# One decoder layer: fewer steps of norm work beside each down-projection tile, a final norm that loads h once, one more step ahead of the broadcasts of a norm, and a weight tile of odd SSM batches in other buffers

## The chip, the cores and the metric

The kernel runs on one core of one Trainium2 chip. The metric is the device time of one execution in microseconds. Three runs of the kernel before gave 2239.86, 2243.06 and 2243.66 us, median 2243.06. The engines are TensorE (PE), VectorE (DVE), ScalarE (ACT), GpSimd (POOL) and SyncE (SP), which issues most of the transfers; each works through its own queue in order, and semaphores tie the queues together.

## The reference

One layer over 2064 tokens (16 meta tokens and 2048), 1024 wide, in float32:

```
hn   = rms_norm(h, norm_mix_g);  proj = hn @ w_in        # b, c, v, u: 512 columns each
conv = b * causal_dwconv3(c * v)
ssm  = g * sigmoid(g @ w_glu),  g = gelu(S5 state space of u)
h    = h + concat(rms_norm(conv), rms_norm(ssm)) @ w_out
up   = causal_dwconv3(rms_norm(h, norm_ffn_g) @ w_up) + bias     # 2 x 2816 columns
h    = h + (silu(a) * val) @ w_down
y    = rms_norm(h, norm_final_g)[meta positions removed]
```

Weights and activations are multiplied as a high part and a low part each, three matmuls for every product: high by high, low by high, high by low.

## The kernel before

The tokens are cut into six pieces of 344, two to a block, and channels lie on the partitions. The program runs through these stages:

1. The input projection of every block, and beside it the SSM in eight batches of four channel groups. For each batch `ssm_load_out` (L699) loads a tile `mo` with the output matrices (512 KB), and `ssm_out` (L772) multiplies it: the matmuls `py` at L781 by `ub` (the input) and at L782 by `sb` (the states that VectorE has scanned). ScalarE evicts them with the gelu into `gb`, and `gb` goes out to DRAM as `g_d`.
2. The first half of the output projection of block 0, whose operands come from the convolution (`pk`, in `conv_part`, eight tiles of 24 matmuls). Meanwhile `g_d` comes back by tokens as four tiles `gt`. ScalarE and VectorE make its high and low parts `gh`, `gl` (L970), and the half-GLU (`glu_block`) multiplies them by `w_glu` into `pg`.
3. The norms of the SSM and conv outputs (names with `ms` and `mc`), the output projection of the three blocks (`po`), and the residual, which `xr` collects and which is written to DRAM as `h_d`.
4. The MLP, three blocks one after the other. `up` does one of 22 pairs of 128 rows of w_up in seven products (matmuls at L1349 to L1351 into `xy` and `pz`, evictions `z`, from L1387 on), then the conv, silu and product. The pairs come in chunks of 4, 4, 4, 3, 3 and 4. After the first pair of a chunk the eight down tiles (`dn`) of the chunk before it are multiplied, evicted (`ev`, L1446) and added to `h_d` by an accumulating transfer.
5. The final norm of a block (`finish`), beside the MLP of the next, and for block 2 at the end (`finish_last`).

A norm is a generator. It squares the input, sums over features with a matmul by ones (`st`, L188), takes the power on GpSimd and multiplies the identity by the result on VectorE (`dg`, three pieces, L203). A matmul by ones then spreads the rows over all partitions (`sb`, L206), and ScalarE copies that out (`rs`). `inv_rms_from` (L214) first loads its input from `h_d` into tiles `sq_f` or `sq_y`, and ScalarE squares them in place.

Such generators wait in a queue called `prep`. The main code calls `prep.step(n)` at fixed places, between projection tiles and after a down tile, and every step runs the generator up to its next `yield`. The number of yields between two parts of a norm therefore sets how much main work lies between them. A second number, the lanes, says how many generators go on in one step. The scheduler then puts each engine's instructions in the order of these calls, as far as the data allow.

Weights are loaded ahead through SP into raw tiles (`wr`), and split by a copy on ScalarE (`wh`, L247) and a subtraction on VectorE (`wl`, L109). Line 109 is the helper for all tensor-tensor operations on VectorE.

Buffers are named by tag and handed on in turn. The tag `sq` has four buffers in the MLP; the loads of the norms, the y tiles and the operands of the next block use them. The tag `ut` has two buffers, through which u is written to DRAM in the first stage.

Of the kernel before, what the change touches and what calls it, by code (L numbers as in the profile page):

```python
# [17 lines left out]
P = 128  # L18
# [39 lines left out]
def layer_kernel(ctx, tc, xq, pk, w_in, w_glu, w_out, w_up, w_down, ssm_s, ssm_m, y):  # L58
# [49 lines left out]
    def tt(out, a, b, op):  # L108
        V.tensor_tensor(out, a, b, op=op)  # L109
# [83 lines left out]
    def inv_rms_at(ss, starts, nfeat, n, name, out=None, keep=False):  # L193
# [8 lines left out]
        for j, o in enumerate(starts):  # L202
            V.tensor_scalar(dg[:sl, o : o + sl], ident[:sl, :sl], r[:sl, j : j + 1], None, op0=ALU.mult)  # L203
        yield
        pb = aux_tile(f"sb_{name}")
        T.matmul(pb[:, :n], ones[:sl, :], dg[:sl, :n], start=True, stop=True)  # L206
# [7 lines left out]
    def inv_rms_from(srcs, n, name, out=None):  # L214
# [6 lines left out]
        yield  # L221
        if xg is not None:
            yield
            yield
        for t in ts:
# [65 lines left out]

    prep, ssm = Side(), Side()
    SQ = 2

# [404 lines left out]
    def ssm_load_out(b):  # L699
        g0 = b * GB  # L700
        mo = a1.tile([P, GB, 2, P], F32, tag="mo", name=f"mo_{b}")
        dma(out=mo, in_=mat_d[:, g0 : g0 + GB, 1:3, :])
        mos[b] = mo

# [68 lines left out]
    def ssm_out(b):  # L773
# [3 lines left out]
        for q in range(PB):  # L777
            ps = mm_tile(f"py_{b}_{q}")
            for par in range(2):
                g = 2 * q + par  # L780
                T.matmul(ps[:, par, :NC], mo[:, g, 1, :], ub[:, g, :], start=True, stop=False)  # L781
                T.matmul(ps[:, par, :NC], mo[:, g, 0, :], yy[b][:, q, par, :], start=False, stop=True)  # L782
            S.activation(gb[:, 2 * q : 2 * q + 2, :], ps[:, :, :NC], AF.Gelu_apprx_tanh)
# [251 lines left out]
    prep.add(prep_glu(0, hg[0]), prep_glu(1, hg[1], **xh2))  # L1035
    prep.lanes = 1
    kept = conv_part(0)
# [259 lines left out]
    def finish(b):  # L1297
        for c in range(2):
            s0, n = y_at(b, c)
            srcs = [h_d[:, i * 4 : i * 4 + 4, s0 : s0 + n] for i in range(2)]  # L1300
            rs = yield from inv_rms_from(srcs, n, f"y{b}{c}")
            yield
            for i in range(2):
                a = half_tile(n, f"y_{b}_{c}_{i}", tag="sq", bufs=4)
                dma(out=a, in_=srcs[i])
                yield
                yield
                for k in range(4):
# [27 lines left out]
    for b in range(3):  # L1336
# [119 lines left out]
        for ci, (f0, nk) in enumerate(chunk_of):  # L1456
# [3 lines left out]
            for f in range(f0, f0 + nk):  # L1460
                up(f, f == f0 + nk - 1 and ci == last)
                if f == f0 and ci:
                    for ms in first_pair:
                        down(ci - 1, ms)
                        work()
                        prep.step(2 * len(ms))
            if ci == last:
# [122 lines left out]
```

## Time and profile before

| | us |
|---|---|
| median of three runs | 2243.06 |
| lowest, highest | 2239.86, 2243.66 |
| the profiled execution | 2245.62 |
| its span in the trace | 2243.8 |
| PE, DVE, ACT, POOL busy in it | 2136.4, 1678.8, 1107.1, 151.6 |

Times in the traces count from the start of the span. A line of the list of waits names who waited, for whom, the total, how many times and the longest. A line of the windows table gives, for a stretch of the span, the busy time and the instructions of each engine, then the clock that was granted to TensorE as a share of its full speed, and the share and rate of the transfers. In the timeline, the brackets hold the idle time of the engine before an instruction and what ended it. Names drop their numbers there: `z` stands for every z tile.

### The profile page before, as it was taken

To read this page: it belongs to the slowest core of one execution; us is meant where nothing else is said; L and a number is where in the kernel's file an instruction comes from. 1 tells how busy PE (TensorE), PEld (TensorE's weight loads), DVE (VectorE), ACT (ScalarE), POOL (GpSimd) and SP (SyncE) were. 2 spreads that over 40 slices of the span, in tenths; PEclk is the share of its full clock that TensorE was granted. 3 is DMA by queue.
4 is the path that set the end of the run, shared out by engine and by line. 5 is a ranking of instruction groups with operands and counts; after the bars stand their busy time and mean duration, and the time that the engine had idled before them with its cause. 6 is when DMAs were issued, how large, how long until landed. Compare 5 with 4: busy or idle time off the path is not lost.

```text
span 2243.8 us, 33100 instructions
## 1 busy us (share of the span) xinstructions
PE 2136.4 (95%) x13012; PEld 2072.6 (92%) x13012; DVE 1678.8 (75%) x2495; ACT 1107.1 (49%) x1647; POOL 151.6 (7%) x174
## 2 busy tenths in 40 slices
PE   4999999999899999999999898999999999999997
PEld 3999999989899999999999898999998999999996
DVE  7776498867866797686669686787768779667776
ACT  3234343326523364554556555455555655555554
POOL 0000000000000001101110010100110010110000
PEclk8899999999999999999999999999999999999998
DMA  5475544343376436525554454725554463554463
GB/s 189 119 225 151 144 133 160 129 130 118 107 245 209 139 95 148 122 77 123 131 131 99 135 148 133 202 77 123 129 133 120 126 180 100 131 119 97 101 174 101
DMA packets 174909, 305.85 MB, mean 136 GB/s; under 512 B 32480, under 2 KB 108960, under 8 KB 174624
## 3 DMA queue, kind: packets, MB, share of 16 engines
q1 hardware_dynamic: 154016, 251.98, 36.2%
q0 software_dynamic: 19584, 47.52, 12.6%
q10 hardware_dynamic: 1152, 4.23, 0.5%
q8 instruction: 102, 1.67, 0.3%
q14 instruction: 55, 0.45, 0.1%
HBM read 219.86 MB, written 83.82 MB: 135 GB/s over the span
## 4 chain that ended last, share of the span: by engine, by line
PE 47%; issue 31%; DVE 8%; DMA 7%; POOL 3%; ACT 2%; SPq 0%; POOLq 0%; DVEq 0%; ACTq 0%
PE xy L1349 5%; PE xy L1350 4%; PE xy L1351 4%; PE dn L138 3%; PE dn L139 3%; POOL h_d L1450 3%; PE dn L142 3%; PE pz L1351 2%; PE pz L1350 2%; PE pz L1349 2%; PE po L138 1%; PE po L139 1%; PE po L142 1%; PE pu L139 1%; PE pu L142 1%
## 5 line engine op out<-in xcount | busy, mean ns | idle before, releaser
L109 DVE TENSOR_TENSOR wl_up<-wr_up,wh_up 128x1024 fp32r<-128x1024 f32 x198 | 241.8, 1222 | 155.0 <-ACT wh_up L247 153.1
L138 PE MATMUL dn<-ah,wh_dn 128*128 128x344 f32 (+1 forms) x1024 | 326.9, 323 | 11.7 <-ACT ah L247 8.9
L139 PE MATMUL dn<-al,wh_dn 128*128 128x344 f32 (+1 forms) x1024 | 325.3, 321 | 0.1
L247 ACT ACTIVATE wh_up<-wr_up 128x1024 fp32r<-128x1024 f32 x198 | 209.3, 1058 | 215.1 <-DVE wr_up L109 59.6
L1349 PE MATMUL xy<-h_t,wh_up 128*128 128x344 f32 (+1 forms) x792 | 264.8, 334 | 11.7 <-ACT z L1387 7.3
L1350 PE MATMUL xy<-l_t,wh_up 128*128 128x344 f32 (+1 forms) x792 | 254.9, 322 | 0.0
L1351 PE MATMUL xy<-h_t,wl_up 128*128 128x344 f32 (+1 forms) x792 | 254.6, 321 | 0.0
L142 PE MATMUL dn<-ah,wl_dn 128*128 128x344 f32 (+1 forms) x1024 | 247.1, 320 | 0.0
L138 PEld LDWEIGHTS dn<-ah,wh_dn 128*128 128x128 f32 x1024 | 193.7, 190 | 16.8 <-ACT ah L247 9.7
L1450 POOL DMA_DIRECT2D h_d<-ev x136 | 118.1, 869 | 1271.6 <-ACT ev L1446 1268.3
L139 PEld LDWEIGHTS dn<-al,wh_dn 128*128 128x128 f32 x1024 | 193.9, 189 | 1.3 <-DVE al L109 0.8
L1349 PE MATMUL xy<-h_b,wh_up 128*128 128x344 f32 (+1 forms) x528 | 176.6, 336 | 10.5 <-ACT ev L1446 8.1
L1349 PEld LDWEIGHTS xy<-h_t,wh_up 128*128 128x128 f32 x792 | 150.5, 190 | 30.4 <-ACT z L1394 13.6
L142 PEld LDWEIGHTS dn<-ah,wl_dn 128*128 128x128 f32 x1024 | 177.9, 189 | 0.0
L1350 PE MATMUL xy<-l_b,wh_up 128*128 128x344 f32 (+1 forms) x528 | 169.8, 322 | 0.0
L1351 PE MATMUL xy<-h_b,wl_up 128*128 128x344 f32 (+1 forms) x528 | 168.6, 321 | 0.0
L1350 PEld LDWEIGHTS xy<-l_t,wh_up 128*128 128x128 f32 x792 | 150.9, 191 | 0.0
L1351 PEld LDWEIGHTS xy<-h_t,wl_up 128*128 128x128 f32 x792 | 150.8, 190 | 0.0
L247 ACT ACTIVATE wh_dn<-wr_dn 128x512 fp32r<-128x512 f32 (+1 forms) x144 | 85.5, 594 | 123.5 <-issue 43.5
L115 DVE SCALAR_TENSOR_TENSOR g<-z,pv,g 128x688 f32<-128x688 f32 (+1 forms) x132 | 122.4, 927 | 19.6 <-ACT g L1354 18.9
L109 DVE TENSOR_TENSOR wl_dn<-wr_dn,wh_dn 128x512 fp32r<-128x512 f32 (+1 forms) x144 | 92.5, 645 | 50.8 <-ACT wh_dn L247 49.8
L115 DVE SCALAR_TENSOR_TENSOR v<-z,pneg,v 128x688 f32<-128x688 f32 (+1 forms) x132 | 122.5, 928 | 9.4 <-ACT v L1354 8.2
(394 smaller groups left out, 5377.2 us busy)
## 6 DMA issues: line engine op xcount, KB each, us to landing
wr_up<-in_w_up SPq DMA_DIRECT2D x132, 512.0 KB, 5.2
h_d<-ev POOLq DMA_DIRECT2D x88, 344.0 KB, 7.0
wr_dn<-in_w_down SPq DMA_DIRECT2D x96, 256.0 KB, 2.7
wr_cw<-in_w_in SPq DMA_DIRECT2D x36, 512.0 KB, 4.7
h_d<-ev POOLq DMA_DIRECT2D x48, 336.0 KB, 6.5
x_c<-in_xq SPq DMA_DIRECT2D x16, 688.0 KB, 4.8
wr_dn<-in_w_down SPq DMA_DIRECT2D x48, 192.0 KB, 2.4
xr<-in_xq SPq DMA_DIRECT2D x24, 344.0 KB, 3.9
```

The source lines that it names most:

```text
L109: V.tensor_tensor(out, a, b, op=op)
L115: V.scalar_tensor_tensor(out=out, in0=a, scalar=s, in1=b, op0=ALU.mult, op1=ALU.add)
L138: T.matmul(ps[c], hi[:, k, :], xh, start=k == 0, stop=False)
L139: T.matmul(ps[c], hi[:, k, :], xl, start=False, stop=False)
L142: T.matmul(ps[c], lo[:, k, :], xh, start=False, stop=k == nk - 1)
L247: S.activation(hi, t, AF.Copy)
L1349: T.matmul(ps, hi[:, j, :], xh[:, j, :], start=start and j == 0, stop=False, **kw)
L1350: T.matmul(ps, hi[:, j, :], xl[:, j, :], start=False, stop=False, **kw)
L1351: T.matmul(ps, lo[:, j, :], xh[:, j, :], start=False, stop=j == 3, **kw)
L1450: G.dma_start(out=h_d[:, m, s0 : s0 + no], in_=ev, accum_op=ALU.add)
```

## The change

There are five edits:

1. `mo` of the odd batches is held in two tiles of tag `ut`, for two groups each, and loaded by two transfers; the even batches keep the tile `mo`.
2. A flag `slack`, set at the start of the second stage, adds one `yield` between `dg` and the `sb` matmul in every norm from there on.
3. `inv_rms_from` always yields four times between the issue of its loads and the Squares. Before, it did so only once the MLP's buffers were open, and yielded twice ahead of that.
4. `finish` loads each half of h once, into y tiles, and writes the squares into separate tiles `ysq`, all of tag `sq`. Before, it loaded h into `sq_y`, squared it in place, and loaded h a second time for the scaling. Eight loads fewer are issued.
5. After a down tile beside the next chunk, `prep.step` runs `len(ms)` steps, no longer twice as many.

```
     def inv_rms_at(...):
             V.tensor_scalar(dg[:sl, o : o + sl], ident[:sl, :sl], r[:sl, j : j + 1], None, op0=ALU.mult)
         yield
+        if slack:
+            yield
         pb = aux_tile(f"sb_{name}")
...
     def inv_rms_from(...):
         yield
         yield
-        if xg is not None:
-            yield
-            yield
+        yield
+        yield
         for t in ts:
             S.activation(t, t, AF.Square)
...
     def ssm_load_out(b):
         g0 = b * GB
-        mo = a1.tile([P, GB, 2, P], F32, tag="mo", name=f"mo_{b}")
-        dma(out=mo, in_=mat_d[:, g0 : g0 + GB, 1:3, :])
-        mos[b] = mo
+        if b % 2 == 0:
+            mo = a1.tile([P, GB, 2, P], F32, tag="mo", name=f"mo_{b}")
+            dma(out=mo, in_=mat_d[:, g0 : g0 + GB, 1:3, :])
+            mos[b] = [mo[:, g] for g in range(GB)]
+            return
+        mos[b] = []
+        for i in range(0, GB, 2):
+            t = cvp.tile([P, NJ, 86], F32, tag="ut", bufs=2, name=f"mo_{b}_{i}").rearrange("p j x -> p (j x)")
+            mo = t[:, : 4 * P].rearrange("p (g m c) -> p g m c", g=2, m=2)
+            dma(out=mo, in_=mat_d[:, g0 + i : g0 + i + 2, 1:3, :])
+            mos[b] += [mo[:, 0], mo[:, 1]]
...
-    prep.lanes = 1
+    prep.lanes, slack = 1, True
     kept = conv_part(0)
...
     def finish(b):
         for c in range(2):
             s0, n = y_at(b, c)
-            srcs = [h_d[:, i * 4 : i * 4 + 4, s0 : s0 + n] for i in range(2)]
-            rs = yield from inv_rms_from(srcs, n, f"y{b}{c}")
-            yield
-            for i in range(2):
-                a = half_tile(n, f"y_{b}_{c}_{i}", tag="sq", bufs=4)
-                dma(out=a, in_=srcs[i])
+            xs, sq = ([half_tile(n, f"{k}_{b}_{c}_{i}", tag="sq", bufs=4) for i in range(2)] for k in ("y", "ysq"))
+            for i, a in enumerate(xs):
+                dma(out=a, in_=h_d[:, i * 4 : i * 4 + 4, s0 : s0 + n])
+            for _ in range(4):
                 yield
-                yield
+            for a, q in zip(xs, sq):
+                S.activation(q, a, AF.Square)
+            yield
+            q = sq[0]
+            tt(q, q, sq[1], ALU.add)
+            tt(q[:, 0:2, :], q[:, 0:2, :], q[:, 2:4, :], ALU.add)
+            tt(q[:, 0, :], q[:, 0, :], q[:, 1, :], ALU.add)
+            yield
+            rs = yield from inv_rms_of(q[:, 0, :], D, n, f"y{b}{c}")
+            yield
+            for i, a in enumerate(xs):
                 for k in range(4):
                     V.scalar_tensor_tensor(
...
                         work()
-                        prep.step(2 * len(ms))
+                        prep.step(len(ms))
```

The first place where the order moves is SP's queue at the end of the SSM. `mo_7` is the tile of the last batch, `ub_7` its input, `wr_o` weights of the output projection, `wr_g` those of the GLU, `gt` the gelu's output on its way back. Before:

```order
L696 DMA ub_7_4174<-u_d_69 128x1032
L702 DMA mo_6_4176<-mat_d_74 128x4x256
L119 DMA wr_o004_4341<-in_w_out 128x512
L119 DMA wr_o005_4476<-in_w_out 128x512
L884 DMA mx_d_71<-tc_2_3_4308 128x2x344
L119 DMA wr_o006_4508<-in_w_out 128x512
L702 DMA mo_7_4417<-mat_d_74 128x4x256
L257 DMA x_mc4_0_5691<-mx_d_71 128x4x344
L963 DMA gt_4465<-g_d_70 128x8x258 x4
L119 DMA wr_o007_4541<-in_w_out 128x512
```

After:

```order
L119 DMA wr_o003_4260<-in_w_out 128x512
L698 DMA ub_7_4180<-u_d_69 128x1032
L712 DMA mo_7_0_4423<-mat_d_74 128x2x256
L712 DMA mo_7_2_4425<-mat_d_74 128x2x256
L119 DMA wr_o004_4347<-in_w_out 128x512
L119 DMA wr_o005_4484<-in_w_out 128x512
L894 DMA mx_d_71<-tc_2_3_4314 128x2x344
L119 DMA wr_o006_4516<-in_w_out 128x512
L258 DMA x_mc4_0_5699<-mx_d_71 128x4x344
L119 DMA wr_o007_4549<-in_w_out 128x512
L973 DMA gt_4473<-g_d_70 128x8x258 x4
```

The two halves of mo_7 now stand right behind ub_7, ahead of wr_o004 to wr_o006, and wr_o007 stands ahead of the four gt loads.

The second place is VectorE in the glu stage, where the norm of the third conv piece (`mc2`) meets that of the first two SSM pieces (`ms0`, `ms1`): `t` is a scaled tile, `l` its low part, `gt` the product with the sigmoid `sg`. Before:

```order
L982 SCALAR_TENSOR_TENSOR t_ms0_5046<-gt_4465,pv_84,rs_ms0_5032 128x344 x2
L982 SCALAR_TENSOR_TENSOR t_ms1_5055<-gt_4465,pv_84,rs_ms1_5036 128x344 x4
L109 TENSOR_TENSOR l_ms0_5052<-t_ms0_5046,h_ms0_5051 128x4x8x43
L203 TENSOR_SCALAR dg_mc2_5064<-ident_75,sr_mc2_5043 115x115 x2
L109 TENSOR_TENSOR gt_4465<-gt_4465,sg_1_3_5099 128x8x86
L109 TENSOR_TENSOR l_ms1_5061<-t_ms1_5055,h_ms1_5060 128x4x8x43
L203 TENSOR_SCALAR dg_mc2_5064<-ident_75,sr_mc2_5043 115x115
L109 TENSOR_TENSOR gt_4465<-gt_4465,sg_2_0_5148 128x8x86
```

After:

```order
L992 SCALAR_TENSOR_TENSOR t_ms0_5092<-gt_4473,pv_84,rs_ms0_5048 128x344 x2
L203 TENSOR_SCALAR dg_mc2_5054<-ident_75,sr_mc2_5043 115x115 x2
L992 SCALAR_TENSOR_TENSOR t_ms0_5092<-gt_4473,pv_84,rs_ms0_5048 128x344
L203 TENSOR_SCALAR dg_mc2_5054<-ident_75,sr_mc2_5043 115x115
L992 SCALAR_TENSOR_TENSOR t_ms0_5092<-gt_4473,pv_84,rs_ms0_5048 128x344
L992 SCALAR_TENSOR_TENSOR t_ms1_5101<-gt_4473,pv_84,rs_ms1_5052 128x344 x3
L109 TENSOR_TENSOR gt_4473<-gt_4473,sg_1_3_5089 128x8x86
L992 SCALAR_TENSOR_TENSOR t_ms1_5101<-gt_4473,pv_84,rs_ms1_5052 128x344
L109 TENSOR_TENSOR l_ms0_5098<-t_ms0_5092,h_ms0_5097 128x4x8x43
L109 TENSOR_TENSOR l_ms1_5107<-t_ms1_5101,h_ms1_5106 128x4x8x43
L109 TENSOR_TENSOR gt_4473<-gt_4473,sg_2_0_5147 128x8x86
```

All three pieces of dg_mc2 now stand ahead of both l_ms. In the same way xr of the fourth output tile now stands ahead of l_ms2 and l_ms3.

The third place is ScalarE in block 2 of the MLP, at the last down tiles of the first chunk and the sixth pair (number 5). `ysq_1_1` are the squares of the second half of block 1; `z_2_5_0` and `z_2_5_1` are evictions of the pair. Before:

```order
L1446 ACTIVATE ev_2_0_6_17232<-dn_2_0_6_0_17203 128x688
L247 ACTIVATE wh_up2_5_3_17260<-wr_up2_5_1_17066 128x1024
L1446 ACTIVATE ev_2_0_7_17266<-dn_2_0_7_0_17235 128x688
L1387 ACTIVATE z_2_5_0_17274<-xy_2_5_17276 128x344
L1356 ACTIVATE z_2_5_1_17275<-halo_z_6795 128x2
L247 ACTIVATE wh_up2_6_0_17305<-wr_up2_6_0_17106 128x1024
L1389 ACTIVATE z_2_5_1_17275<-pz_2_5_1_17278 128x344
```

After:

```order
L1464 ACTIVATE ev_2_0_6_17225<-dn_2_0_6_0_17196 128x688
L1316 ACTIVATE ysq_1_1_0_17269<-y_1_1_0_17267 128x4x344
L248 ACTIVATE wh_up2_5_3_17258<-wr_up2_5_1_17064 128x1024
L1464 ACTIVATE ev_2_0_7_17264<-dn_2_0_7_0_17233 128x688
L1405 ACTIVATE z_2_5_0_17273<-xy_2_5_17275 128x344
L1374 ACTIVATE z_2_5_1_17274<-halo_z_6803 128x2
L1316 ACTIVATE ysq_1_1_1_17270<-y_1_1_1_17268 128x4x344
L248 ACTIVATE wh_up2_6_0_17304<-wr_up2_6_0_17106 128x1024
L1407 ACTIVATE z_2_5_1_17274<-pz_2_5_1_17277 128x344
```

The two Squares now stand among the evictions. ysq_1_1_0 takes the buffer of y_1_0_0, and ysq_1_1_1 that of y_1_0_1, so each waits for the write of that y tile to DRAM. The same happens in block 1 with ysq_0_1, and in block 1 again at pair 9, where the load of sq_f21_1 takes the buffer of a y tile, and its Square stands between ev_1_1_7 and z_1_9_0.

More of the change, by code (lines that the diff above doesn't have):

```diff
@@ L292, in layer_kernel @@
     prep, ssm = Side(), Side()
+    slack = False
     SQ = 2
@@ L780, in ssm_out @@
                 g = 2 * q + par
-                T.matmul(ps[:, par, :NC], mo[:, g, 1, :], ub[:, g, :], start=True, stop=False)
-                T.matmul(ps[:, par, :NC], mo[:, g, 0, :], yy[b][:, q, par, :], start=False, stop=True)
+                T.matmul(ps[:, par, :NC], mo[g][:, 1, :], ub[:, g, :], start=True, stop=False)
+                T.matmul(ps[:, par, :NC], mo[g][:, 0, :], yy[b][:, q, par, :], start=False, stop=True)
             S.activation(gb[:, 2 * q : 2 * q + 2, :], ps[:, :, :NC], AF.Gelu_apprx_tanh)
```

## The prediction

> **What bounds the kernel now.** I read the page first, for the balance of the engines.
>
> ```profile
> span 2243.8 us, 33100 instructions
> PE 2136.4 (95%) x13012; PEld 2072.6 (92%) x13012; DVE 1678.8 (75%) x2495; ACT 1107.1 (49%) x1647; POOL 151.6 (7%) x174
> ```
>
> TensorE works for 2136.4 of 2243.8 us, and the change takes no matmul away. What it can win or lose lies in the 107 us in which TensorE stands, and in what a stall does to the pace behind it. So the second view was the list of TensorE's waits (total us, how many, the longest), cut here to those near the edits:
>
> ```profile
> PE xy L1349 <- ACT z L1387: 7.3, 2, 6.8
> PE py L781 <- DMA mo<-mat_d: 5.3, 1, 5.3
> PE sb_mc L206 <- DVE dg_mc L203: 4.0, 2, 3.8
> PE po L138 <- DVE xr L109: 3.7, 1, 3.7
> PE st_f L188 <- DVE sq_f L109: 3.4, 1, 3.4
> PE pk L142 <- DVE wl_o L109: 1.9, 1, 1.9
> PE sb_y L206 <- DVE dg_y L203: 1.1, 2, 0.7
> ```
>
> Third, the table by windows of 4 us, around each of these waits (us, busy time and instructions of PE, PEld, DVE, ACT, POOL, then granted clock, DMA share, GB/s). A full window looks like the one at 496: 27 records, two of them cut by its edges, so 25 matmuls or 0.16 us each.
>
> ```profile
> 488.00:492.00 4.00, 2.87 (x7) 2.44 (x8) 2.87 (x6) 0.00 (x0) 0.00 (x0) 0.50 0.84 319
> 492.00:496.00 4.00, 4.00 (x16) 3.37 (x16) 0.00 (x0) 1.11 (x2) 0.00 (x0) 0.74 0.00 0
> 496.00:500.00 4.00, 4.00 (x27) 4.00 (x26) 0.53 (x1) 1.29 (x3) 0.00 (x0) 1.00 0.33 134
> ...
> 524.00:528.00 4.00, 3.54 (x13) 3.55 (x14) 3.83 (x4) 4.00 (x4) 0.00 (x0) 0.60 0.41 131
> ...
> 572.00:576.00 4.00, 2.17 (x6) 1.72 (x7) 3.70 (x5) 0.58 (x2) 0.00 (x0) 0.58 0.00 0
> 576.00:580.00 4.00, 4.00 (x17) 4.00 (x17) 3.73 (x6) 2.89 (x4) 0.00 (x0) 0.57 0.38 96
> ...
> 616.00:620.00 4.00, 2.37 (x8) 2.40 (x9) 4.00 (x7) 0.71 (x1) 0.00 (x0) 0.62 0.54 159
> 620.00:624.00 4.00, 4.00 (x16) 4.00 (x16) 4.00 (x5) 1.06 (x1) 0.00 (x0) 0.52 0.95 289
> ...
> 706.00:710.00 4.00, 3.09 (x13) 3.09 (x14) 2.68 (x7) 0.00 (x0) 0.85 (x1) 0.50 0.89 265
> 710.00:714.00 4.00, 4.00 (x20) 4.00 (x19) 0.22 (x1) 1.35 (x2) 0.00 (x0) 0.68 0.68 212
> ...
> 1360.00:1364.00 4.00, 3.82 (x13) 3.83 (x14) 3.11 (x5) 1.60 (x5) 0.86 (x1) 0.50 0.60 142
> ```
>
> After each stall the granted clock stands near 0.5 for some microseconds, and the busy time holds too few matmuls. At full pace the busy time of a window would hold 27 × (busy / 4); what is missing, at 0.16 us each, is the price of the clock. Mo: (19.4 - 7) + (27 - 16) = 23.4 missing, 3.7 us, so 5.3 + 3.7 = **9.0**. Pk: 23.9 - 13 = 10.9, 1.7 us, **3.6** in all. Sb_mc: 8.6 + 10 = 18.6, 3.0 us, **6.8**. Po: 8 + 11 = 19, 3.0 us, **6.7**. St_f: 7.9 + 7 = 14.9, 2.4 us, **5.8**. Z: 25.8 - 13 = 12.8, 2.0 us, **8.8**.
>
> That is 40.7 us of stalls that the edits touch. The rest of the list is left alone.
>
> *The row against the rule.* A stall of 1.9 us (pk) is followed by a clock of 0.60, so I charge the clock for short stalls too. The Trainium skill, "TensorE: Matmul & The Clock Gate", Part 1 on the clock gate, says that the clock halves after an idle window of about 3.4 us, with windows that run freely. The trace does not agree in that length. By that rule the three charges of 1.5 us that I make below for new short waits would be nothing, and the sum an estimated -13.6 instead of -9.1.
>
> **Part one: the SSM stage, mo and the glu stage.** Five rows of the timeline tell what is late next (start, duration, engine, line, operation; in brackets the idle time before it and who ended it):
>
> ```profile
> 490.25 0.69 DVE L109 TENSOR_TENSOR sb<-zi,zr 64x514 f32<-64x514 f32 x1
> ...
> 494.62 0.60 ACT L783 ACTIVATE gb<-py 128x516 f32<-128x516 f32 x1 [10.19 <-PE py L782]
> ...
> 570.89 2.61 DVE L109 TENSOR_TENSOR l_ms<-t_ms,h_ms 128x1376 fp32r<-128x1376 f32 x1
> 573.43 0.26 DVE L203 TENSOR_SCALAR dg_mc<-ident,sr_mc 115x115 f32<-115x115 f32 x1
> ...
> 609.58 5.74 DVE L109 TENSOR_TENSOR l_ms<-t_ms,h_ms 128x1376 fp32r<-128x1376 f32 x2 [1.56 <-ACT h_ms L987]
> ...
> 616.63 0.85 DVE L109 TENSOR_TENSOR xr<-po,xr 128x688 f32<-128x688 f32 x1
> ```
>
> The last mo load goes from SP's place 158 to places 157 and 158, ahead of three weight loads, into buffers free early, so its wait goes. But py_7 also needs sb, whose last piece ends at 490.9. In the new order 24 pk matmuls (3.8 us) stand ahead of that, so TensorE fills most of the gap. The gelu evictions come at about 491.6 instead of 494.62, 3 us earlier, and with them g_d, gt, gh, gl. Wh_o007 now stands ahead of gh on ACT, so the pk wait goes as well.
>
> In the glu stage dg_mc sat behind an l_ms of 2.61 us, and xr<-po behind two of 5.74 us. Both now stand ahead of them, so the sb_mc and po waits should go. TensorE's load thus falls by 9.0 + 3.6 + 6.8 + 6.7 = 26.1 us. The time does not, since this stage is nearly as full on VectorE. One row of the windows table takes it from the first gl to the last of the xr's:
>
> ```profile
> 517.50:628.00 110.50, 100.05 (x581) 96.43 (x580) 100.59 (x124) 66.97 (x66) 6.08 (x6) 0.92 0.36 110
> ```
>
> VectorE is busy for 100.59 of 110.5 us, and its work there does not shrink. So the stage can win at most the 3.7 us or so of an earlier start and the 9.9 us of VectorE's idle time: 13.6. It wins nothing if other waits take the place of these. I take 3 us of start and half the idle time, 5: **-8** (0 to -13.6).
>
> **Part two: the norm ahead of the MLP.** With four yields in every case between load and Square, st_f00 moves about one output tile (3.8 us) later on TensorE, past its wait of 3.4 us. All of it could go, 5.8. The same delay pushes the first MLP operands towards the end of the out-projection, where no later work covers them: I take **-4** (0 to -5.8). The extra yield behind dg_y does the same for 1.1 us: **-0.5** (0 to -1.1).
>
> **Part three: the final norm.** Eight loads of 672 to 688 KB go. They kept the queues full, but no matmul waits for one of them, so they count only through what lands sooner. Price and place of the new order come from these rows: ACT ahead of the z that TensorE waits 6.8 us for, VectorE's scaling, the chain's transfers (start, time to land), the medians of issues to landing.
>
> ```profile
> 1356.85 1.35 ACT L226 ACTIVATE sq_f<-sq_f 128x1376 f32<-128x1376 f32 x1 [10.06 <-DMA sq_f<-h_d]
> 1358.11 1.04 ACT L247 ACTIVATE wh_up<-wr_up 128x1024 fp32r<-128x1024 f32 x1
> 1359.05 0.72 ACT L1446 ACTIVATE ev<-dn 128x688 f32<-128x688 f32 x1
> 1359.68 0.45 ACT L1387 ACTIVATE z<-xy 128x344 f32<-128x344 f32 x1
> ```
>
> ```profile
> 1328.30 2.97 DVE L1309 SCALAR_TENSOR_TENSOR y<-y,pv,rs_y 128x336 f32<-128x336 f32 x6 [0.63 <-ACT rs_y L211]
> ...
> 1333.55 0.69 DVE L109 TENSOR_TENSOR wl_dn<-wr_dn,wh_dn 128x512 fp32r<-128x512 f32 x1 [2.28 <-ACT wh_dn L247]
> ```
>
> ```profile
> 1335.23 8.97 DMA out_y<-y
> 1344.22 12.61 DMA sq_f<-h_d
> ...
> 1415.67 3.59 DMA out_y<-y
> 1419.28 5.45 DMA sq_f<-h_d
> ```
>
> ```profile
> out_y<-y SPq DMA_DIRECT2D x4, 688.0 KB, 4.7
> ...
> out_y<-y SPq DMA_DIRECT2D x4, 672.0 KB, 6.1
> ```
>
> ACT takes its queue in order: a Square that waits for a transfer holds the weight split, the eviction and z behind it, and TensorE waits for z. The new order has this form three times, since a Square's output takes the buffer of a y that is being written out.
>
> *Blocks 1 and 2, up 5.* Sb_y now follows the fifth of eight down tiles; call its end T. The first y is scaled at about T + 6.3 (1.5 for the copy and the way there, my estimate; four scalings at 0.5; four weight operations of 0.7 between them) and lands L later. Square, split, eviction and z take 1.35 + 1.04 + 0.72 + 0.45 = 3.6. TensorE needs z after 97 matmuls, T + 15.5: it waits L - 5.6. The second y leaves 4.1 later, and Square, split and z (2.85) must end by T + 17.9, 112 matmuls on: in all L - 4.7. The medians give 0 to 1.4, the long row of 8.97 gives 4.3. I take L = 7, since the queues are full there but 1.4 MB less is asked of them: 2.3 us and 1.5 of clock, 3.8 at each place. In block 1 this replaces the 8.8: **-5.0** (-8.8 to -2.5, the latter with 2.0 of clock). In block 2 it is new: **+3.8** (0 to +6.3).
>
> *Block 1, up 9.* The Square of sq_f21 follows a load into a buffer that an out_y must first leave. L and the load's M come one after the other: 6.3 + L + M + 1.35 + 0.45 against 15.5, a wait of L + M - 7.4. The rows of this place give 9.0, so 1.6; the pair at 1335 gives 21.6, so 14.2. Nearer to the first: L + M = 10.5, 3.1 and 1.5 of clock, **+4.6** (+1.6 to +16.2).
>
> **The sum.** -8 - 4 - 0.5 - 5.0 + 3.8 + 4.6 = **-9.1**; the best ends give -27.7, the worst +20. The profiled execution took 2245.62 us for its span of 2243.8, so 2236.5 in its terms. It lies 2.6 above the median of 2243.06, so the median should be **2234.0**.
>
> **The rivals.**
> *VectorE holds the early gain (no change).* The waits for dg_mc and xr come back as waits for t, gt or wl of the same queue, since 9.9 us of idle time is all there is. For it speaks the 91% of that row, against it that two stalls come from an order with long operations ahead of short ones. Then -3 - 4 - 0.5 + 3.4 = -4, and with st_f halved -2: about 2241.
> *ACT's new stalls outweigh it (slower).* One mechanism: a Square behind an out_y that lands late. For it speaks the 10.06 us that ACT stood at the Square before, with the queues full; against it the loads that go. At 8.97 and 12.61 it costs -2.5 + 6.3 + 16.2 = +20, with -12.5 before it +7.5: 2250.6. It decides once the three places together cost over 12.5 us, that is at L + M of about 17.
> *All of it comes off.* VectorE's whole idle time is used, the medians hold: -20 and better, under 2223.
>
> **How the numbers follow.** About 0.2%, 4.5 us, is what a measurement of this kernel can tell from no change. The forecast's own case (a gain of 4.5 to 19 us): 0.58. All of it comes off: 0.08. No change: 0.20. Slower: 0.14. So faster 0.66, same 0.20, slower 0.14. The range runs from 2224, a gain of 19, to 2249, 6 above the median, which takes in most of no change and half of the slower case.
>
> **What would show it.** In the profile after: no wait for mo, wl_o, dg_mc, and st_f under 1 us; TensorE's records in 484:496 near 27 in a window but for one gap at 488 to 491; VectorE over 93% busy in the glu stage. In blocks 1 and 2 at up 5, z waits of 1 to 4 us with an ACT Square ended by out_y ahead of them, and one behind sq_f at up 9 of block 1. I am wrong if the glu stage wins under 3 us, if st_f still waits, or if one z wait is over 6 us.

## The result, and the profile after

| | before | changed |
| --- | --- | --- |
| median of 7 runs each, us | 2243.66 (2239.86 to 2247.1) | 2229.66 (2228.1 to 2236.57) |
| ratio to before, 95% interval | | 0.9949 [0.9934, 0.9964] |
| the profiled execution, its span, us | 2245.62, 2243.8 | 2229.58, 2227.8 |
| mean granted clock of TensorE | 0.975 | 0.982 |

The changed kernel is faster. A second measurement of it, among the experiments below, gave 0.9966 [0.9954, 0.9979], a median of 2235.27 beside 2242.51. The forecast was 2234.0 from 2243.06, a ratio of 0.9960, which lies between the two; the gain is 0.3% to 0.5%, some 8 to 11 us.

First the page of the changed kernel: its span, and the busy time of each engine.

```profile
span 2227.8 us, 33100 instructions
PE 2118.0 (95%) x13012; PEld 2056.8 (92%) x13012; DVE 1674.7 (75%) x2495; ACT 1108.9 (50%) x1647; POOL 151.0 (7%) x174
```

TensorE does the same 13012 matmuls. Before, it was busy for 2136.4 us and idle for 2243.8 - 2136.4 = 107.4; now it is busy for 2118.0 and idle for 109.8. **The idle time has not shrunk. All of the gain is busy time**: the same matmuls at a better clock. The mean granted clock bears it out: 2243.8 x 0.975 and 2227.8 x 0.982 are both 2187.7, so in sum the clock alone sets the two executions apart. To see where, the span is cut at six pairs of places, found by setting the start of the same matmul in both traces side by side, so that each window holds the same matmuls. The table by windows of before (us, busy time and records of PE, PEld, DVE, ACT, POOL, then granted clock, DMA share, GB/s):

```profile
0.00:460.00 460.00, 421.68 (x2516) 408.57 (x2517) 356.03 (x749) 169.52 (x193) 11.40 (x16) 0.96 0.52 155
460.00:740.00 280.00, 260.68 (x1546) 252.85 (x1545) 197.97 (x265) 120.13 (x120) 12.76 (x12) 0.95 0.50 163
740.00:1181.00 441.00, 436.12 (x2742) 424.42 (x2741) 329.36 (x430) 239.00 (x377) 36.97 (x42) 1.00 0.47 120
1181.00:1687.00 506.00, 486.81 (x2977) 472.73 (x2976) 382.82 (x503) 276.73 (x473) 45.41 (x52) 0.98 0.50 131
1687.00:2048.00 361.00, 351.63 (x2162) 341.62 (x2161) 276.30 (x352) 197.57 (x312) 29.46 (x34) 0.99 0.49 126
2048.00:2243.80 195.80, 179.47 (x1079) 172.39 (x1077) 136.30 (x201) 104.16 (x175) 15.56 (x18) 0.95 0.48 126
```

And of the changed kernel:

```profile
0.00:455.90 455.90, 416.84 (x2516) 403.24 (x2517) 356.03 (x749) 169.40 (x193) 11.40 (x16) 0.97 0.53 157
455.90:730.20 274.30, 254.50 (x1546) 245.78 (x1545) 192.59 (x260) 118.88 (x119) 12.64 (x12) 0.98 0.52 166
730.20:1167.70 437.50, 433.71 (x2742) 422.80 (x2741) 333.87 (x435) 240.80 (x378) 36.68 (x42) 1.00 0.48 120
1167.70:1671.30 503.60, 483.93 (x2977) 470.78 (x2976) 381.07 (x503) 277.63 (x473) 45.24 (x52) 0.98 0.49 126
1671.30:2034.65 363.35, 352.34 (x2162) 344.48 (x2161) 274.86 (x352) 198.20 (x312) 29.50 (x34) 0.98 0.46 117
2034.65:2227.80 193.15, 176.71 (x1079) 169.76 (x1077) 136.27 (x201) 104.00 (x175) 15.58 (x18) 0.96 0.50 128
```

Row by row the changed kernel takes 4.1 us less up to the end of the SSM's first batches, 5.7 less from there to the end of the output projection (the SSM's end, glu, the norm ahead of the MLP), 3.5 less in block 0, 2.4 less in block 1, 2.35 more in block 2 and 2.65 less in the tail. In the second row TensorE's idle time is 280 - 260.68 = 19.3 before and 274.3 - 254.5 = 19.8 after, while its busy time falls by 6.2: the stage of the prediction's first two parts wins by the clock alone. The first row is mostly luck, shown under the experiments.

The list of TensorE's waits of the changed kernel, cut to those near the edits (total us, how many, the longest), says what became of the stalls:

```profile
PE xy L1367 <- ACT z L1405: 7.5, 2, 7.0
PE st_mc L188 <- DVE sq_mc L109: 5.4, 2, 4.9
PE st_ms L188 <- DVE sq_ms L109: 2.4, 2, 1.8
PE pg L142 <- DVE wl_g L109: 2.2, 1, 2.2
PE po L138 <- DVE xr L109: 1.9, 1, 1.9
PE st_f L188 <- DVE sq_f L109: 1.3, 2, 1.0
```

Mo (5.3) and the pk behind wl_o (1.9) are gone, sb_mc is down to 0.3, po to 1.9, st_f to 1.3. In their place stand st_mc, st_ms and wl_g, with some shorter ones: other names, nearly the same sum. The table in windows of 4 us of the changed kernel shows what the new stalls did to the clock:

```profile
572.00:576.00 4.00, 3.82 (x15) 3.85 (x16) 3.52 (x5) 0.00 (x0) 0.94 (x1) 0.50 0.67 228
...
616.00:620.00 4.00, 4.00 (x18) 4.00 (x18) 4.00 (x6) 1.06 (x1) 0.00 (x0) 0.60 1.02 318
```

Before, five stalls of this stretch were each followed by a clock near half: at 488, 524, 572, 616 and 706. Now two are, at 572 and 616. The second profile of the changed kernel shows the same two places and no other. Five pieces of idle time became more and shorter pieces. Behind the short ones, at 484 and (wl_g) at 518, the clock stays at 1.00 with 27 records in the windows 488:492 and 520:524. The wl_g stall of 2.2 us is longer than the 1.9 us of before at 524, which was followed by 0.60; the paragraph on the clock shows what told them apart.

### The profile page after: what moved, and what is told of

It is laid out like the page before. It is cut to its first block, busy times and chain, and to the rows that moved or that the text cites. A ratio compares the mean times of both kernels' runs of the same rounds, so it can differ in the third digit from the quotient of the medians.

```text
span 2227.8 us, 33100 instructions
## 1 busy us (share of the span) xinstructions
PE 2118.0 (95%) x13012; PEld 2056.8 (92%) x13012; DVE 1674.7 (75%) x2495; ACT 1108.9 (50%) x1647; POOL 151.0 (7%) x174
## 5 line engine op out<-in xcount | busy, mean ns | idle before, releaser
L1367 PE MATMUL xy<-h_b,wh_up 128*128 128x344 f32 (+1 forms) x528 | 176.6, 335 | 12.5 <-ACT z L1414 11.0
```

Source lines behind the costliest of these rows:

```text
L1367: T.matmul(ps, hi[:, j, :], xh[:, j, :], start=start and j == 0, stop=False, **kw)
```

## The experiments

All ratios are against the kernel before on the same chip, in five rounds for the experiments. TensorE's idle and busy time are from each kernel's page, with 13012 matmuls in every one. They belong to one execution each, which lies up to 5 us from its kernel's median.

| kernel | median us | ratio, 95% interval | idle us | busy us |
| --- | --- | --- | --- | --- |
| before | 2242.51 to 2243.66 | 1 | 107.4 | 2136.4 |
| changed, first measurement | 2229.66 | 0.9949 [0.9934, 0.9964] | 109.8 | 2118.0 |
| changed, again | 2235.27 | 0.9966 [0.9954, 0.9979] | 107.3 | 2123.6 |
| mo alone | 2239.91 | 0.9984 [0.9975, 0.9993] | 106.6 | 2130.0 |
| all yields of the norms alone | 2251.54 | 1.0043 [1.0031, 1.0055] | 120.0 | 2134.4 |
| final norm and single steps alone | 2245.74 | 1.0009 [1.0, 1.0018] | 112.5 | 2131.9 |
| mo and single steps, no yields | 2251.88 | 1.0038 [1.0025, 1.0051] | 115.1 | 2134.9 |
| changed, old final norm | 2232.74 | 0.9957 [0.9942, 0.9972] | 106.3 | 2123.6 |
| changed, no mo | 2239.97 | 0.9982 [0.9968, 0.9995] | 111.7 | 2126.5 |
| changed, double steps | 2234.5 | 0.996 [0.9945, 0.9975] | 104.0 | 2123.8 |
| changed, no extra yield in the MLP | 2238.89 | 0.9987 [0.9977, 0.9997] | 105.6 | 2128.5 |
| changed, Square two steps later | 2235.04 | 0.9968 [0.9956, 0.998] | 108.8 | 2128.2 |
| changed, short writes | 2231.15 | 0.9946 [0.993, 0.9961] | 101.7 | 2127.7 |
| changed, old norm for block 1 | 2233.37 | 0.9952 [0.9939, 0.9966] | 108.9 | 2122.6 |

The columns read well together: where a kernel is slower than before, its idle time is up by 8 to 13 us; where it is faster, its busy time is down by 6 to 18. The final norm alone has 5 more of the one and 4.5 less of the other, and comes out even.

**One part alone: mo.** The kernel before with the change's `ssm_load_out` and nothing else.

```
-        mo = a1.tile([P, GB, 2, P], F32, tag="mo", name=f"mo_{b}")
+        if b % 2 == 0: ...
+        for i in range(0, GB, 2):
+            t = cvp.tile([P, NJ, 86], F32, tag="ut", bufs=2, name=f"mo_{b}_{i}")...
...
```

> The kernel before with the mo edit alone. My theory, that VectorE holds most of what this stage wins: the mo wait of 5.3 us and the wl_o wait of 1.9 us go, but the waits for dg_mc and xr in the glu stage stay or grow, and the net gain is 3 to 4.5 us, 0.998 to 0.9985 of the time before. Rival one, each stall is worth its own price (5.3 + 3.7 and 1.9 + 1.7): a gain of 12.6 us, 0.9944. Rival two, the GLU takes all of it back: no gain, 1.000.

Measured 0.9984 [0.9975, 0.9993], 3.6 us, as my theory had it. The stage row, cut at the same matmuls as above, and the list of TensorE's waits of this kernel:

```profile
459.00:734.70 275.70, 255.86 (x1546) 247.36 (x1545) 197.38 (x265) 120.23 (x120) 12.76 (x12) 0.98 0.50 164
```

```profile
PE sb_mc L206 <- DVE dg_mc L203: 4.6, 3, 3.8
PE st_f L188 <- DVE sq_f L109: 3.8, 1, 3.8
PE po L138 <- DVE xr L109: 3.6, 1, 3.6
PE pg L142 <- DVE wl_g L109: 2.4, 1, 2.4
```

The mo wait of 5.3 is gone and a new wl_g of 2.4 has come, while the other three stand nearly as before. The stage wins 4.3 us: the idle time is 275.7 - 255.86 = 19.8, as before, and the busy time is 4.8 less. What mo's stall and its clock would give (9.0 by the prediction's prices, 12.6 with pk) is more than twice that. The stall's own time is taken back by shorter stalls, and the clock's part stays won.

**One part alone: the yields of the norms.** The kernel before with the extra yield behind dg and the four yields in `inv_rms_from`; the final norm and the steps as before.

```
+        if slack:
+            yield
...
-        if xg is not None:
-            yield
-            yield
+        yield
+        yield
...
```

> The kernel before with the extra yield behind dg and the four yields in every inv_rms_from, without the mo edit, the new final norm and the thinner steps. My theory: dg_mc and xr stand ahead of the long l_ms, st_f has its tile, VectorE's queue caps the first: a gain of 4 to 7 us, 0.997 to 0.998. Rival one, each stall is worth its own price (6.8 + 6.7 + 5.8): a gain of 19 us, 0.9914. Rival two, other waits of the same queue take their place: under 2 us, 0.999 to 1.001.

Measured 1.0043 [1.0031, 1.0055], slower by 9.6 us: my theory falls, and no rival had it either. The stage up to the MLP wins only 0.45 us in this profile:

```profile
461.50:741.05 279.55, 257.43 (x1546) 249.03 (x1545) 192.68 (x260) 118.65 (x119) 12.62 (x12) 0.96 0.50 164
```

Its busy time is 3.2 less than before, its idle time 2.8 more. Blocks 1 and 2 lose 7.7 and 4.7. One place of it is SP's queue in block 2 (start, duration, operation):

```profile
1841.96 1.97 SPq L1314 DMA_DIRECT2D out_y<-y  x2
1855.56 0.37 SPq L1307 DMA_DIRECT2D y<-h_d  x1
1856.02 12.70 SPq L1255 DMA_DIRECT2D wr_up<-in_w_up  x3
```

The old final norm loads h a second time into the buffer of a y that is on its way out. With the extra yield that load comes behind both writes, so SP stands for 1855.56 - 1843.93 = 11.6 us until one has landed, and three weight loads stand behind it. The timelines of VectorE, ScalarE and TensorE show who pays: the sums of weights on VectorE that wait for such a load, a weight split behind them for which ScalarE stands 6.48 us, with a z behind it, and TensorE.

```profile
1863.80 1.42 DVE L109 TENSOR_TENSOR wr_up<-wr_up,wr_up 128x512 f32<-128x512 f32 x2 [4.42 <-DMA wr_up<-in_w_up]
1866.06 1.06 ACT L248 ACTIVATE wh_up<-wr_up 128x1024 fp32r<-128x1024 f32 x1 [6.48 <-DVE wr_up L109]
```

```profile
1867.51 0.43 PE L1351 MATMUL xy<-h_b,wh_up 128*128 128x344 f32 x1 [4.29 <-ACT z L1398]
```

**One part alone: the final norm.** The kernel before with the new `finish` and `prep.step(len(ms))`.

```
+            xs, sq = ([half_tile(n, ...) for i in range(2)] for k in ("y", "ysq"))   # shortened
...
-                        prep.step(2 * len(ms))
+                        prep.step(len(ms))
```

> The kernel before with the new final norm and the thinner steps alone. My theory: block 1 at up 5 loses its wait of 6.8 us, new Squares behind out_y cost about the same in the other two places, so the net lies between -3 and +3 us, 0.9987 to 1.0013. Rival, the eight loads that go relieve the queues and that is most of the gain of the whole change: a gain of 8 us or more, under 0.9965.

Measured 1.0009 [1.0, 1.0018]: no gain alone, as my theory had it. The profile bears no simple sum, though: in it block 0 wins 3.3 us and block 1 loses 7.2.

**The extra yield in the MLP.** The changed kernel, with the extra yield switched off where the MLP begins.

```
-    xp_, SQ = fp, 4
+    xp_, SQ, slack = fp, 4, False
```

> The changed kernel with the extra yield switched off again when the MLP begins; nothing else. The broadcast of the final norm, its scaling and its writes come one down tile (3.8 us) earlier, and so do the Squares behind them. My theory, the z waits at up 5 of blocks 1 and 2 and at up 9 (3.3, 3.1 and 7.0 us in the profile) are the time that out_y lands too late, so each shrinks by up to 3.8 us: 5 to 9 us faster than the changed kernel, about 0.991 to 0.993 of before. Rival, the Square only stands among earlier evictions and stalls those by as much: within 2 us of the changed kernel, 0.994 to 0.996.

Measured 0.9987 [0.9977, 0.9997], by the ratios 0.2% behind the changed kernel's second measurement, whose interval it just overlaps, and 0.4% behind its first: the yield looks worth more than I or the rival gave it. Without it the z wait at up 5 of block 1 is 4.33, and the stalls move to evictions: at 1435.28 TensorE waits 7.49 us for an ev.

The kernel of the paragraph above (final norm alone), which has the same order in the MLP, shows 8.46 where this one shows 4.33. The load that the Square waits for landed in 10.3 us there (1340.82 to 1351.1) and in 6.2 here (1335.72 to 1341.9). So one profile of one order does not fix the price of such a wait.

**The changed kernel again.** No edit; on the chip of the next kernels.

> The changed kernel once more, as the yardstick for its neighbours here, and for one question: in its first profile TensorE ran 3.6 us ahead of before by 100 us, where both queues still hold the same instructions. My theory: that is where the clock fell after the same stalls, by chance; here the lead at 100 us lies between -1 and +4 us, the ratio between 0.993 and 0.9965. Rival: the lead is the change's own and is 3.6 us again.

Measured 0.9966 [0.9954, 0.9979], at the edge of what my theory gave. At 100 us into the span this execution stands within 0.06 us of before, where the first one led by 3.6. Nothing of the program differs there. One row of the windows of before:

```profile
98.00:102.00 4.00, 4.00 (x18) 3.94 (x17) 3.62 (x34) 1.15 (x3) 0.00 (x0) 0.55 0.72 215
```

The same window of the changed kernel's first profile:

```profile
98.00:102.00 4.00, 4.00 (x28) 3.74 (x27) 2.45 (x6) 2.32 (x4) 0.00 (x0) 1.00 0.91 247
```

TensorE is busy for all of both windows, with the same kind of matmuls, and ran at another clock. Of the 4.1 us of the first stage 3.6 are chance, and a single profile's stage is sure to 2 or 3 us only.

**The Square at up 9.** The changed kernel, with two more steps between load and Square for the second half of a block.

```
-            for _ in range(4):
+            for _ in range(4 + 2 * c):
```

> The changed kernel with two more yields ahead of the Squares of the second half in the final norm. On ScalarE only one thing moves: the Square of sq_f21_1 stands behind the evictions of pair 9 of block 1 instead of ahead of the first. My theory: the z wait of 7.0 us there and the clock behind it go, 5 to 8 us faster than the changed kernel of the same call, 0.991 to 0.993 of before. Rival: the same load is waited for by the next in line, within 2 us of the changed kernel.

Measured 0.9968 [0.9956, 0.998], the same as the changed kernel: the rival had it. The z wait of 7.0 at up 9 goes, and two others come: 4.38 us for a z of VectorE at 1444.49, and 4.63 us for an ev at 1588.57.

**Short writes.** The changed kernel, with `out_y` of blocks 0 and 1 cut to 43 columns; most of those two blocks' outputs stay unwritten.

```
-                dma(out=y[:, i * 4 : i * 4 + 4, s0 - META : s0 - META + n], in_=a)
+                dma(out=y[:, i * 4 : i * 4 + 4, s0 - META : s0 - META + 43], in_=a[:, :, :43])
```

> The changed kernel with 43 columns of each y tile of the final norm's first two blocks written out instead of all (this leaves most of those outputs unwritten). My theory: the Squares at up 5 wait for out_y to land, so the z waits of 3.3 and 3.1 us fall under 1 us, and that of 7.0 at up 9 by about the 4 us that out_y takes there: 7 to 12 us faster than the changed kernel of the same call. Rival: full queues and the loads hold them, not the writes: under 3 us faster.

Measured 0.9946 [0.993, 0.9961], 4.1 us below the changed kernel on the same chip, between the two theories, though the two intervals overlap a little. TensorE's timeline at the three places:

```profile
1343.01 0.42 PE L1367 MATMUL xy<-h_t,wh_up 128*128 128x344 f32 x1 [2.02 <-ACT z L1405]
...
1436.68 0.65 PE L1367 MATMUL xy<-h_t,wh_up 128*128 128x344 f32 x1 [6.52 <-ACT z L1405]
...
1836.85 0.43 PE L1367 MATMUL xy<-h_t,wh_up 128*128 128x344 f32 x1 [1.90 <-ACT z L1405]
```

At the two up 5 the wait falls from 3.3 and 3.1 to about 2: there the landing of the write is part of it. At up 9 it stays at 6.5, as in the second profile of the changed kernel. There the write of 43 columns lands 3.6 us after its issue, but the load of sq_f stands behind a weight load in SP's queue (issued at 1424.22 and 1424.64), so that it leaves 4.2 us after the write, and it takes another 10.3 us to the Square at 1434.93: the load holds this place.

**The changed kernel with the old final norm.**

```
-            xs, sq = ...
+            srcs = [h_d[:, i * 4 : i * 4 + 4, s0 : s0 + n] for i in range(2)]
+            rs = yield from inv_rms_from(srcs, n, f"y{b}{c}")
...
```

> The changed kernel with the old final norm (h loaded twice, Squares in place); mo, the yields and the thinner steps stay. No Square then takes the buffer of a y that is written out at up 5, and that of sq_f21_1 stands behind the evictions of pair 9. My theory: the second load costs nothing and the three new waits (3.3, 3.1, 7.0 us) are the price of the new final norm, so this is 5 to 12 us faster than the changed kernel of the same call, 0.989 to 0.993 of before. Rival: the eight loads that come back fill the queues, and the wait of 6.8 us at up 5 of block 1 comes back with them: 3 us slower than the changed kernel or more.

Measured 0.9957 [0.9942, 0.9972], not to be told from the changed kernel, and what neither theory had: once yields, single steps and mo are in, reading h once is worth nothing that can be measured. There is no wait at up 9 then, and one of 6.9 at another place. In SP's queue at the place shown above the second load stands ahead of the second write, and it does not hold the queue:

```profile
1836.51 0.38 SPq L1315 DMA_DIRECT2D y<-h_d  x1
1837.46 0.68 SPq L1322 DMA_DIRECT2D out_y<-y  x1
```

**Mo and single steps, without the yields.** The kernel before with those two edits.

```
+        (ssm_load_out as in the change)
-                        prep.step(2 * len(ms))
+                        prep.step(len(ms))
```

> The kernel before with mo and the thinner steps alone: the old final norm, no extra yields. Against mnt_old_finish it lacks only the norm's yields, which alone made the kernel slower by 0.43%. My theory now: with thinner steps the yields are worth 1 to 4 us, and mo (3.6 us) with the thinner steps in block 0 (2 to 3 us) makes most of the gain, so 0.996 to 0.998 of before. Rival: the yields carry the gain once the steps are thin, so without them only mo is left, 0.998 to 1.000.

Measured 1.0038 [1.0025, 1.0051]. My theory falls, and the rival had too little of the size: without the yields, mo and single steps cost what with them they win. Its waits on z add up to 9.8, 7.9 and 5.1 us over three lines, and in SP's queue the y load again comes 10 us behind two writes (1849.64 after 1836.86 + 2.34).

**Double steps.** The changed kernel with the fifth edit undone.

```
-                        prep.step(len(ms))
+                        prep.step(2 * len(ms))
```

> The changed kernel with the double steps beside the down tiles back; all else stays. The Squares of the final norm then stand ahead of four down evictions and the first z's instead of one. My theory: the yields only pay with thin steps, since with double ones the Squares wait for loads among the evictions, so this loses 4 to 12 us on the changed kernel, 0.999 to 1.003 of before. Rival: the thinness is worth nothing, within 2 us of the changed kernel, 0.995 to 0.9975.

Measured 0.996 [0.9945, 0.9975], the same as the changed kernel. With the new final norm the pace of the steps is worth nothing; the rival had it.

**The changed kernel without mo.**

```
-        if b % 2 == 0: ...
+        mo = a1.tile([P, GB, 2, P], F32, tag="mo", name=f"mo_{b}")
+        dma(out=mo, in_=mat_d[:, g0 : g0 + GB, 1:3, :])
...
```

> The changed kernel without the mo edit. My theory: mo is worth in it what it is worth alone, 3 to 4.5 us, so 0.9975 to 0.9985 of before. Rival: the glu stage with its norms ahead of the long operations makes mo worth its whole stall, 9 to 12.6 us, 1.000 or more.

Measured 0.9982 [0.9968, 0.9995], as expected: by the ratios mo is worth 3.6 to 7.4 us inside the change, by the second measurement what it is worth alone.

**The old norm for block 1 alone.** The changed kernel, where block 1's final norm (which runs beside block 2) is the old one.

```
...   # finish_twice is the old norm
-            prep.add(finish(b))
+            prep.add(finish(b) if b == 0 else finish_twice(b))
```

> The changed kernel with the old final norm (two loads of h) for block 1 alone, that is beside block 2 of the MLP, where the new one added a z wait of 3.1 to 3.3 us and the old one had none over 0.7. My theory: 2 to 5 us faster than the changed kernel, 0.993 to 0.995 of before, and no z wait over 1 us at up 5 of block 2. Rival: the start of block 2 takes it back (its two waits there of 4.3 and 0.7 us), within 1.5 us of the changed kernel.

Measured 0.9952 [0.9939, 0.9966]. The z wait at up 5 of block 2 is gone, and at the start of block 2 stand waits of 3.80 and 1.54 us where the changed kernel has one of 5.09. None of the versions is clearly better than the changed kernel; this one and it cannot be told apart, which leaves my theory and the rival undecided.

Set out by the two edits that meet in the MLP, the ratios show that they do not add up:

| | no extra yields | with the yields |
| --- | --- | --- |
| old final norm, double steps | 0.9984 (with mo) | 1.0043 (without mo) |
| old final norm, single steps | 1.0038 (with mo) | 0.9957 (with mo) |
| new final norm, single steps | 1.0009 (without mo) | 0.9949, 0.9966 (with mo), 0.9982 (without) |
| new final norm, double steps | not run | 0.996 (with mo) |

Mo is worth 0.0016 to 0.0033 wherever it was tried. With the old norm the yields cost at double steps and win 0.8%, 18 us, at single steps; with the new norm they win some 0.3% and the steps do nothing.

## Why the prediction was right, and where its steps failed

The total came out as forecast, faster by a third to half of a per cent, and in part that was luck: its two halves were off in opposite directions. The stage up to the MLP won less than half of what was forecast, the MLP won where it was to lose, and some of the first measurement's lead is the chance at 100 us.

**What bounds the kernel.** TensorE, as said; but the reading that its 107 us of idle time is what can be won failed. That time is 109.8 and 107.3 us in the two profiles of the changed kernel. What was won was the other half of each price, the clock.

**Part one, -8, and part two, -4 and -0.5.** Together -12.5; the stage gave -5.7 and, in the second profile, -5.1. Eight profiles that share these edits up to the MLP gave 3.1 to 7.7. Mo alone gave -4.3 in its profile, the norms' yields alone -0.45. Cut at both ends of the prediction's row of the glu stage, so that each window again holds the same matmuls, the stage shows where the forecast went wrong. The stretch ahead of the glu stage, before:

```profile
460.00:517.50 57.50, 52.16 (x299) 50.06 (x298) 25.71 (x39) 18.20 (x24) 0.00 (x0) 0.94 0.51 168
```

The same stretch of the changed kernel, and behind it the glu stage, with the same 581 matmuls as the 110.5 us of before:

```profile
455.90:507.05 51.15, 49.96 (x299) 48.17 (x298) 26.37 (x39) 16.51 (x24) 0.00 (x0) 1.00 0.54 178
507.05:619.75 112.70, 97.88 (x581) 93.98 (x580) 98.39 (x121) 68.71 (x65) 5.95 (x6) 0.95 0.37 112
```

Ahead of the glu stage 6.35 us are won, where 3 were forecast: of mo's stall 1.2 us are left, as a wait for sb. All ten profiles with the mo edit (the changed kernel has two) win 6.3 to 6.4 us there, and the three without it nothing. The glu stage, which was to win 5, is 2.2 us longer (2.1 in the second profile), and TensorE's idle time in it rose from 10.5 to 14.8. All ten with mo lose 1.1 to 4.1 us there; the three without it lie between 1.5 us won and 0.1 lost. From there to the MLP, where st_f and the first MLP operands lie, 1.5 us are won (0.8 in the second profile).

So the step that failed is that half of VectorE's idle time in the glu stage would come off: in place of +5 us won, 2.2 were lost, and the sign "the glu stage wins under 3 us" came true against me. The size of the early start, 3, was too small by half, and that of part two, 4.5, too large. VectorE shows it in a row from the first gl to the same xr as in the prediction's row:

```profile
510.98:619.08 108.10, 93.28 (x552) 89.39 (x551) 97.69 (x120) 65.74 (x64) 5.95 (x6) 0.95 0.37 112
```

97.69 of 108.1 is 90%, no more than the 91% of before, where I had named 93% as the sign. By these ends of VectorE's own the stretch is 2.4 us shorter, but with 4 of its 124 records and 29 of the 581 matmuls no longer in it: they now stand behind it. In the larger windows above, VectorE has 5.4 us less up to the MLP and 4.5 more in block 0. And the order that freed dg_mc made another wait. VectorE's timeline at the place where sb_mc's stall was:

```profile
560.77 6.20 DVE L109 TENSOR_TENSOR l_ms<-t_ms,h_ms 128x1376 fp32r<-128x1376 f32 x2 [0.66 <-ACT h_ms L997]
...
571.50 0.53 DVE L109 TENSOR_TENSOR sq_mc<-sq_mc 128x344 f32<-128x344 f32 x1
```

The two l_ms of 6.20 us that dg_mc no longer stands behind are ahead of the next piece's sq_mc now. TensorE's timeline has the bill, 4.91 us where sb_mc's was 3.8:

```profile
572.18 1.29 PE L188 MATMUL st_mc<-ones,sq_mc 128*115 128x1 f32 x6 [4.91 <-DVE sq_mc L109]
```

That is the rival "VectorE holds the early gain". What it lacked is the clock, which paid in its stead: five slow stretches became two. By the prediction's counting of missing matmuls those five cost 13.8 us and the two cost 2.8 + 1.7 = 4.5, while the busy time fell by 6.2; what took back the other 3 us is not shown. St_f fell from 3.4 to 0.4 and 1.0 us, so it still waits, but no slow stretch follows it any more.

**Part three, the three places.** The form was as described: a Square held by a transfer, and z behind it. ScalarE's timeline of the changed kernel:

```profile
1429.92 1.35 ACT L227 ACTIVATE sq_f<-sq_f 128x1376 f32<-128x1376 f32 x1 [7.56 <-DMA sq_f<-h_d]
...
1834.90 1.35 ACT L1316 ACTIVATE ysq<-y 128x1376 f32<-128x1376 f32 x1 [3.38 <-DMA out_y<-y]
```

And TensorE's:

```profile
1340.97 0.42 PE L1367 MATMUL xy<-h_t,wh_up 128*128 128x344 f32 x1 [3.34 <-ACT z L1412]
...
1431.66 0.65 PE L1367 MATMUL xy<-h_t,wh_up 128*128 128x344 f32 x1 [6.96 <-ACT z L1405]
...
1838.03 0.66 PE L1367 MATMUL xy<-h_t,wh_up 128*128 128x344 f32 x1 [3.13 <-ACT z L1412]
```

*Up 5, blocks 1 and 2* (2.3 us each forecast): 3.34 and 3.13. The step held: the second write of each place took 8.3 and 8.0 us to land, where I took 7 for L, and L - 4.7 is 3.6 and 3.3. The clock of 1.5 was charged for both: behind 3.34 us it stayed at 1.00, behind 3.13 it fell to 0.72 and 0.85.

*Up 9, block 1* (3.1 us forecast): 6.96. The mechanism was right and one size was off. SP issued the write, a weight load and the load of sq_f:

```profile
1414.84 0.39 SPq L1330 DMA_DIRECT2D out_y<-y  x1
1418.90 0.33 SPq L1263 DMA_DIRECT2D wr_up<-in_w_up  x1
1420.29 0.38 SPq L221 DMA_DIRECT2D sq_f<-h_d  x1
```

L is 1420.29 - 1414.84 = 5.45, near the 3.59 and 4.7 to 6.1 that I had. The write landed after 5.4 us, but the weight load between them left SP only after 4.1, so little of L is the write's alone. M, from 1420.29 to the Square at 1429.92, is 9.6, where the row that I leaned on had 5.45. By the formula L + M - 7.4 is 7.7, beside 6.96 measured, where I had 3.1. The row of 12.61 was the nearer one. So the sign "one z wait over 6 us" that would prove me wrong came true, and yet the time did not follow it: taking this wait away (the Square two steps later) brought two others and changed nothing.

**What was in no term.** The MLP was to lose 3.4 us and won 6.2 (and 6.5 in the second profile). Block 2 lost 2.35 where +3.8 was forecast; the rest was missing. The tail won 2.65, and this is the extra yield: the nine profiles with it in the MLP win 1.7 to 2.8 us there, the four without it 0.5 to 0.9. Block 0 won 3.5, 1.1 of it idle time, in the middle of the block; all kernels with single steps or the new norm have 1.7 to 3.5 there, the two without have 0.25 and 0.7. And in block 1, which won 2.4 where -0.4 was forecast, three waits at its start, of 3.8, 2.1 and 1.2 us, became one of 5.6.

**The clock.** The prediction named the Trainium skill, "TensorE: Matmul & The Clock Gate", Part 1, by which the clock halves after an idle window of about 3.4 us, of windows that run freely, and an estimated sum of -13.6 with it. The traces agree in the windows and not in the idle time that it takes. In all fourteen traces the granted clock is 1.00 or 0.50 for whole pieces of 3.41 us, whose borders keep one beat from the start of the execution to its end. Cut at these borders, the windows table of the changed kernel shows the stalls of 3.34 and 3.13 us:

```profile
1336.01:1339.42 3.41, 1.62 (x11) 1.34 (x9) 0.20 (x1) 1.56 (x2) 0.00 (x0) 1.00 0.98 229
1339.42:1342.83 3.41, 1.86 (x12) 1.86 (x13) 3.41 (x4) 1.50 (x4) 0.00 (x0) 1.00 0.51 112
...
1834.35:1837.77 3.42, 0.55 (x4) 0.27 (x2) 1.49 (x1) 2.87 (x5) 0.00 (x0) 1.00 0.87 194
1837.77:1841.18 3.41, 3.15 (x11) 3.15 (x12) 3.41 (x6) 0.21 (x1) 0.00 (x0) 0.50 0.02 6
```

A border splits the longer stall into 1.79 and 1.55 us of idle time, and the clock stays at 1.00 in the next piece too. The shorter one puts 2.87 us into one piece, and the next is at 0.50. The second profile of the changed kernel has the first of these stalls, 3.35 us there, with 3.04 us of it in one piece, and there the clock halves. In the same way the 1.9 us of before at 524 lie in one piece, and the 2.2 us at 518 of the changed kernel are split into 1.16 and 1.08. From 460 to 2050 us of the fourteen traces, 6130 pieces at 1.00 had under 1.3 us of idle TensorE, and none of them was followed by 0.50; 116 had over 1.9 us, and all of them were; of the 73 between, 24 were. So stalls well under 3.4 us can cost clock, as the prediction charged, but whether one does depends on how much of it falls into one piece, which changes from one execution to the next. A charge of 1.5 us for every short wait was too much, and none at all would be too little. That also fits the five slow stretches that became two: fewer pieces hold so much idle time when it comes in shorter stalls.

**What stays open.** Why yields and steps win together and lose apart is shown at one place (the y load behind two writes, with the weights behind it), not for the whole of the 18 us. And no order of the three places was found that is clearly better.

## What to carry to other kernels

Split a gain or a loss into the idle and the busy time of the bound engine over windows that hold the same instructions: here the stalls only changed their names, and the clock behind them made the gain. Make sure that the windows do hold the same instructions, by the count of matmuls in them. When a stall is taken from an engine whose feeder is 90% busy, look in the new order for what now stands behind the feeder's long operations, since that is the next stall. A transfer into a buffer that a write must first leave holds all that is queued behind it on its queue, so place it ahead of the next write, and test edits of pace together, not one by one.

## What the runs showed of the hardware that was not expected

- The same stall costs clock in one execution and not in another: 1.59 us at 772 before (0.75, then 0.82 in the windows there), 1.57 us at the same matmul after, with the mean clock of that stretch at 1.00. With the waits beside it the idle time of its 3.41 us piece was 1.96 us before; after, a border split it into 1.28 and 0.94. Near 100 us, ahead of every edit, one profile shows 0.55 and the other 1.00, with TensorE busy throughout; that is not explained.
- Two programs with the same order of the MLP differed by 6.6 us in block 1, 4.1 of it by the time of one load (10.3 and 6.2 us for the same 688 KB).
- The landing of a write was only part of a Square's wait: with the writes cut to 43 columns the waits at up 5 fell by about 1.3 us, and that at up 9 was 6.52, beside 6.96 and 6.47 in the two profiles of the changed kernel.
